# A hybrid decoder layer on one core: the last tile's RWKV tail factored ahead of its norm, four of its output weights in another ring, and the query's token rows on ScalarE's queue

## The chip, the core and the metric

The kernel runs on one core of one Trainium2 chip. A core has five engines with an instruction queue each: TensorE (PE in the profile; its weight loads are PEld), VectorE (DVE), ScalarE (ACT), GpSimd (POOL) and SyncE (SP). Each works through its own queue in order and waits on semaphores. SP, ACT and POOL also issue the DMA transfers. The metric is the device time of one execution in microseconds (us). Before the change it is 3875.11 us, the median of three runs (3873.53, 3875.11 and 3887.86).

## What is computed

One layer of a hybrid decoder, for 1024 prompt tokens and 64 sample tokens (8 sequences of 8), model width 1024. Cut to what matters here:

```python
xn = rmsnorm(h, norm_mix)
proj = xn @ w_in                                # retention columns | RWKV-7 columns
o_ret = head_norm(o_ret, GN_EPS) * silu(g_ret)  # retention, chunks of 128 tokens
gate = sigmoid(fg) @ rw_g2
o_rw = head_norm(o_rw, RWKV_LN_EPS) * rw_ln_g + rw_ln_b
o_rw = o_rw + jnp.sum(r4 * k4 * rw_rk, axis=-1, keepdims=True) * v4
o_rw = o_rw * gate
h = h + jnp.concatenate([o_ret, o_rw], axis=-1) @ w_out
# peer: 8 heads, 2 x 128 keys, the best 16 of each, 16 experts of 16384 per token and head
q = (rmsnorm(h, norm_ffn) @ wq)                 # query, scores against keys, top 16
h = h + sum over experts of gelu(xn . u[e]) * softmax(score) * v[e]
h = h + sigmoid(rmsnorm(h, ple_norm) @ ple_gate) * (p_l @ ple_proj)
y = rmsnorm(h, norm_final)
```

The three lines of `o_rw` that follow the head norm are the ones that the change factors in another way.

## The kernel before, in words

The tokens are cut into nine tiles: 0 to 7 of 128 prompt tokens, and 8 with the 64 sample tokens. The program's author writes generators (a `yield` ends each piece), and a scheduler puts the pieces of all of them into one fixed order for each engine. So the order is not written out by hand: a change of a ring, of a buffer's size or of an engine can move work that has nothing to do with it, also far from the place. All on-chip tiles come from rings: a tag with `bufs` slots. A new tile waits until the reader of the slot's last owner is done; a pool that is laid over the memory of a closed pool waits for its readers in the same way.

The stages, in the order of the program:

- **Projections** (`group_a`) and **mixers** (`ret_mix`, `rw_mix`), tile by tile in the order 0, then 1, 8, 2, 3, 4, 5, 6, 7 (`BORDER`, in `group_b`). The RWKV chain carries a state from tile to tile, so tile 7 ends it. `rw_mix` ends with `py` (the outputs of the 8 heads, in PSUM), the head norm (`head_norm`, L403 to L420), and L970 to L984: times `lng` (L972), plus `lnb` (L973), plus the bonus term `bv` (L975, L976), times the gate `p` (L978 is the matmul, tile `pgt`). For tile 7 the result stays on the chip as `self.tail` (L980, L981), in the ring `Wq`; all of it is VectorE's.
- **Output rows** (`c_rows`, L572 to L631): the rows of `od` are loaded (`cot`), transposed (`etr`, `coT`), multiplied with `w_out` (tiles `cw`, matmuls `ewo`), added to `x` (`ch`), normed with `norm_ffn` (`cgr` holds its row), and written to `xd` in DRAM. For the last tile (`da` is given) all eight `cw` of 128x1024 are loaded into slots of the rings `uh` and `ul` (L581), `ch` into a slot of `uraw`, and the normed rows are split and transposed straight into the query's operand.
- **Early experts** (`early`, `gather`): for tiles 0, 1 and 8 the expert rows are gathered row by row by an indirect DMA that POOL issues (`grow`, L1130), 512 KB a step, and VectorE multiplies them: first with the token (L1144), then into the sum (L1158, tile `gacc`). These steps run all through the mixers and the query, one tile after another. They are put into the order as filler between other work. The early query of a tile uses the ring `Wq` (four slots of 128x1024) for its weights.
- **Query** (`c_query`) for tiles 2 and 3 (operand `x1`) and 4 to 7 (`x`): `rows_in` loads the token rows from `xd` (`cxn`, L1002, a ring of two), transposes them (`ntr`, L321) and splits them into two fp32r parts (`cx`: ScalarE L298, VectorE L300). Then for 16 blocks: weights `wqr` are loaded by SP into `uraw`, split into `wqh` and `wql` (ScalarE, POOL), multiplied (`pq`), scored (`psc`), and the best 16 are picked by VectorE (L1035 to L1039).
- **Gates and hidden units** of tiles 4 to 7 (dense), gathers for tiles 2 and 3, then the dense second half (`py`, L1303), and the last stage (`ple`) with the final norm.

The place of the change is the seam between mixers and query. SP's queue holds there, one behind the other: the token rows `cxn`, the eight `cw`, `ch`, `wqr` and `cgr`. The pool `da` with `uh`, `ul` and `uraw`, and the pool `cn` with `cxn`, are laid over memory that the mixers used.

Of the kernel before, what the change touches and what calls it, by code (L numbers as in the profile page):

```python
# [8 lines left out]
F32 = mybir.dt.float32  # L9
# [5 lines left out]
OP = mybir.AluOpType  # L15
AX = mybir.AxisListType

D = 1024
# [145 lines left out]
UB = 2  # L164
# [15 lines left out]
DW = 4  # L180
# [6 lines left out]
PGT = "a"  # L187
# [7 lines left out]
QB = 4  # L195
# [5 lines left out]
def spans(tiles):  # L201

    e = [sum(SIZE[t] for t in tiles[:i]) for i in range(len(tiles) + 1)]
    return dict(zip(tiles, e)), e[-1]
# [8 lines left out]
class K:  # L213
# [357 lines left out]
    def c_rows(self, wp, t, ring=4, da=None, x=None):  # L571

        nc, I = self.nc, self.I
        n = SIZE[t]
        half = lambda name: wp.tile([128, 512], F32, name=name, tag="x2k", bufs=ring)
        cs = [slice(0, 512), slice(512, 1024)]
        if da is not None:
            ws = []
            for k in range(8):
                ws.append(da.tile([128, D], F32, name="cw", tag=("uh", "ul")[k % 2], bufs=DW))  # L580
                nc.sync.dma_start(ws[k], I['w_out'][k])  # L581
        if da is not None:
            h = da.tile([128, D], F32, name="ch", tag="uraw", bufs=UB)
        else:
            h = wp.tile([128, D], F32, name="ch", tag="sr", bufs=1)
        nc.sync.dma_start(h[:n], I['x'][t * 128:t * 128 + n])
        yield
        ot = [half("cot"), self.tail if t == 7 else half("cot")]
        oT = [wp.tile([128, 4, 128], F32, name="coT", tag="qm", bufs=2) for _ in range(2)]
        for k in range(1 if t == 7 else 2):  # L590
            nc.sync.dma_start(ot[k][:n], self.od[t][:n, cs[k]])
        yield
        for k in range(2):
            p = self.ps("etr", "a").rearrange("p (a b) -> p a b", a=4)
            for j in range(4):
                nc.tensor.transpose(p[:, j, :n], ot[k][:n, j * 128:j * 128 + 128], self.c("ident")[:n, :n])
            nc.scalar.activation(oT[k][:, :, :n], p[:, :, :n], AF.Copy)
            yield
        if da is not None:
            p = [self.ps("ewo", "b") for _ in range(2)]  # L600
            for k in range(8):
                for c in range(2):
                    nc.tensor.matmul(p[c][:n], oT[k // 4][:, k % 4, :n], ws[k][:, cs[c]], start=k == 0, stop=k == 7)
            for c in range(2):
                nc.vector.tensor_tensor(h[:n, cs[c]], p[c][:n], h[:n, cs[c]], op=OP.add)
        else:
            for c in range(2):
                p = self.ps("ewo", "a")
                for k in range(8):
                    w = half("cw")  # L610
                    nc.sync.dma_start(w, I['w_out'][k, :, cs[c]])
                    nc.tensor.matmul(p[:n], oT[k // 4][:, k % 4, :n], w, start=k == 0, stop=k == 7)  # L612
                    if k % 4 == 3:
                        yield
                nc.vector.tensor_tensor(h[:n, cs[c]], p[:n], h[:n, cs[c]], op=OP.add)
        nc.scalar.dma_start(self.hd[t][:n], h[:n])
        junk = wp.tile([128, D], BF, name="csq", tag="x2k", bufs=ring)
        ssq = wp.tile([128, 1], F32, name="cssq")
        nc.scalar.activation(junk[:n], h[:n], AF.Square, accum_out=ssq[:n])
        r = self.rsq(wp, ssq, n, 1.0 / D, 1e-6, 1, "crs")  # L620
        gr = [half("cgr") for _ in range(2)]
        o = ROWS['norm_ffn'][0]
        for c in range(2):
            nc.sync.dma_start(gr[c], I['rows'][o + 512 * c:o + 512 * c + 512].partition_broadcast(128))
            nc.vector.scalar_tensor_tensor(h[:n, cs[c]], h[:n, cs[c]], r[:n], gr[c][:n], op0=OP.mult, op1=OP.mult)
        if x is not None:
            self.split_T(h, n, x[0], x[1], 0)
        else:
            nc.scalar.dma_start(self.xd[t][:n], h[:n])
        self.rowed.add(t)  # L630
        yield  # L631
# [64 lines left out]
    def rw_mix(self, t):  # L696
        nc, I, O, wp = self.nc, self.I, self.O, self.cw
        smp = t == 8
        n, o = SIZE[t], t * 128
# [3 lines left out]
        hb = "bd" if smp or first else "bb"  # L703
        T2 = lambda name: wp.tile([128, 4 * n], F32, name=name, tag="t2", bufs=6)
        T3 = lambda name: wp.tile([128, 512], F32, name=name, tag="t3", bufs=4)
# [7 lines left out]
        p = self.ps("pz")  # L713
# [8 lines left out]
        sf13 = wp.tile([128, 128], F32, name="sf13", bufs=b2)  # L722
# [3 lines left out]
        for k in range(2):  # L726
            p = self.ps("pcs")[:, :258].rearrange("p (a b) -> p a b", a=2)
# [10 lines left out]
        p = self.ps("pa").rearrange("p (a b) -> p a b", a=4)  # L738
# [21 lines left out]
        p = self.ps("pbon")  # L760
# [3 lines left out]
        bon = wp.tile([128, 16], F32, name="bon", bufs=b2)  # L764
# [24 lines left out]
        for src, dst in ((nbt, Q), (kt, Kq)):  # L789
            for k in range(2):  # L790
# [6 lines left out]
                for s in range(2):  # L797
# [4 lines left out]
                    else:  # L802
                        for j in range(2):
                            h = 2 * (2 * k + j) + s
# [3 lines left out]
        for nm, src in (("vtk", vT), ("nbk", nbt), ("ktk", kt)):  # L808
            d = wp.tile([128, 512], F32, name=nm, bufs=b2)
# [21 lines left out]
        for li, m in enumerate(LEVELS):  # L831
# [4 lines left out]
            for s in range(2):  # L836
                p = self.ps("trz", hb[s]).rearrange("p (a b) -> p a b", a=4)
# [4 lines left out]
                p = self.ps("pG", hb[s])[:, :256].rearrange("p (h q) -> p h q", h=4)  # L842
# [5 lines left out]
            for s in range(2):  # L848
                p = self.ps("pZG", hb[s])[:, :256].rearrange("p (h q) -> p h q", h=4)
# [11 lines left out]
        def state_mm(p, hp, j):  # L861
            pr = p[:n, hp * 128:hp * 128 + 128]
            if smp:
                return self.seq_state(self.co, art[:, hp, j, :64], I['s_wkvT'], hp)
            elif not first:
                nc.tensor.matmul(pr, art[:, hp, j, :n], S0[:, hp, :], start=True, stop=False)

        V = toks["vtk"]
        hq = lambda h: (h % 2) * 4 + h // 2
        p = self.ps("pX", "d")  # L870
        for hp in range(4):
            sq = state_mm(p, hp, 0)
            for s in range(2):
                h = 2 * hp + s
# [8 lines left out]
        if smp:  # L883
            p = self.ps("pU", "d")
# [5 lines left out]
        else:  # L890
            lo, up = slice(0, 64), slice(64, 128)
            for half in (lo, up):
                if half is up:
                    p = self.ps("pL", "d")
# [5 lines left out]
                p = self.ps("pU", "d")  # L900
# [5 lines left out]
        if not smp:  # L906
            p = self.ps("pS", "d").rearrange("p (a b) -> p a b", a=4)
# [15 lines left out]
            if t == 7:  # L923
                p = self.ps("pso", "d").rearrange("p (a b) -> p a b", a=4)
# [7 lines left out]
        else:  # L932
# [6 lines left out]
            for h in range(8):  # L939
                hs = slice(h * 64, h * 64 + 64)  # L940
                p = self.ps("pss", "b")
# [16 lines left out]
        for hp in range(4):  # L958
            sq = state_mm(py, hp, 1)
            for s in range(2):  # L960
                h = 2 * hp + s
                hs = slice(h * 64, h * 64 + 64)
                if smp:
                    self.seq_mm(py[:n, hs], *sq, s)
                nc.tensor.matmul(py[:n, hs], Kq[:n, hq(h), 1, :n], V[:n, hs], start=first, stop=False)
                nc.tensor.matmul(py[:n, hs], Q[:n, hq(h), 1, :n], U[:n, hs], start=False, stop=first or smp or s == 1)
            if hp % 2:
                yield
        xc = self.head_norm(wp, py, n, 64e-5, T3)
        xf = xc.rearrange("p h d -> p (h d)")  # L970
        eng = nc.vector if t == 7 else nc.gpsimd
        eng.tensor_tensor(xf[:n], xf[:n], self.lng[:n], op=OP.mult)  # L972
        eng.tensor_tensor(xf[:n], xf[:n], self.lnb[:n], op=OP.add)  # L973
        bv = T3("bv").rearrange("p (h d) -> p h d", h=8)
        nc.vector.tensor_tensor(bv[:n], V[:n].rearrange("p (h d) -> p h d", h=8), bon[:n, 8:16, None].to_broadcast([n, 8, 64]), op=OP.mult)  # L975
        eng.tensor_tensor(xc[:n], xc[:n], bv[:n], op=OP.add)  # L976
        p = self.ps("pgt", PGT or hb[0])
        nc.tensor.matmul(p[:n], sf13[:, :n], self.g2, start=True, stop=True)  # L978
        if t == 7:
            self.tail = self.ep0.tile([128, 512], F32, name="tail", tag="Wq", bufs=QB)  # L980
            nc.vector.tensor_tensor(self.tail, xf, p, op=OP.mult)  # L981
        else:
            nc.vector.tensor_tensor(xf[:n], xf[:n], p[:n], op=OP.mult)
            nc.scalar.dma_start(self.od[t][:n, 512:], xf[:n])  # L984

# [10 lines left out]
    def rows_in(self, wp, tiles, x):  # L996

        off, _ = spans(tiles)
        for t in tiles:
            n = SIZE[t]  # L1000
            xn = wp.tile([128, D], F32, name="cxn", bufs=CN)
            self.nc.sync.dma_start(xn[:n], self.xd[t][:n])  # L1002
            self.split_T(xn, n, x[0], x[1], off[t])
            yield

# [552 lines left out]
```

## Time and profile before

| | |
|---|---|
| median of three runs | 3875.11 us |
| the profiled execution's own time | 3881.51 us |
| its span (first to last instruction) | 3879.7 us |
| busy in the span: PE, PEld, DVE, ACT, POOL | 86%, 71%, 77%, 31%, 61% |
| mean granted TensorE clock | 0.883 of full speed |
| read and written in HBM | 986.68 MB, 95.94 MB |
| gather steps of 512 KB (L1130) | 1152 |
| tail of tile 7 ready (L981 ends) | 1767.8 us |
| first query matmul of tiles 4 to 7 | 1840.6 us |

How to read the rows below. A row of the chain gives the start in us from the span's start, the length, and what ran; the chain is followed back from the last instruction, each step to what released it. A row of the timeline gives start, length, engine, line, operation and shape, and in brackets the idle time before it. A row of the waits gives who waited for whom: us in total, times, the longest. A row of the DMA issues gives the queue, the count, the size of one, and the median us from issue to landing. The table by stretches gives busy us of each engine, the granted clock, the DMA engines' share and what they moved. The lines that carry the prediction are shown in it.

### The profile page before, as it was taken

The numbers are of one execution on the slowest core, as the hardware profiler recorded it, in microseconds if no ns is written. First come the engines' busy times: TensorE is split into PE (matmuls) and PEld (weight loads), VectorE is DVE, ScalarE is ACT, GpSimd is POOL, SyncE is SP. The second block draws the span as 40 slices with busy tenths as digits, with TensorE's granted clock in tenths as the row PEclk, the third lists the DMA queues.
The fourth block names the chain that finished last, engine by engine and source line by source line (L and its number), as shares of the span: only waits on it lengthen the run. The fifth ranks groups of instructions, "written<-read, shape, count | busy, mean of one in ns | idle before, by whom it ended". The sixth has DMA issues, their size and how long they took to land.

```text
span 3879.7 us, 52665 instructions
## 1 busy us (share of the span) xinstructions
PE 3346.4 (86%) x17749; PEld 2748.3 (71%) x17749; DVE 2984.9 (77%) x5884; ACT 1220.5 (31%) x2247; POOL 2361.5 (61%) x2059
## 2 busy tenths in 40 slices
PE   7789995868779878883999989999899989899979
PEld 7688894645747757662887767887688766677757
DVE  4454388877787697876998999977777777788875
ACT  4232220111111111211232626777533333333322
POOL 5363176454365365554569888875688787777740
PEclk9799995667868567876999999999899999999989
DMA  7266558899778878889779888998999999999962
GB/s 249 74 218 208 172 179 285 279 300 296 231 243 285 294 264 272 290 288 327 223 261 309 298 289 316 315 349 320 346 339 339 336 361 359 358 352 345 334 223 72
DMA packets 457320, 1086.23 MB, mean 280 GB/s; under 512 B 73627, under 2 KB 176281, under 8 KB 452378
## 3 DMA queue, kind: packets, MB, share of 16 engines
q0 software_dynamic: 165888, 604.05, 44.4%
q1 hardware_dynamic: 236638, 382.77, 31.0%
q10 hardware_dynamic: 54524, 96.03, 6.6%
q8 instruction: 141, 2.31, 0.2%
q14 instruction: 129, 1.06, 0.1%
HBM read 986.68 MB, written 95.94 MB: 279 GB/s over the span
## 4 chain that ended last, share of the span: by engine, by line
PE 37%; DVE 24%; DMA 12%; POOL 8%; issue 8%; ACT 3%; ACTq 0%; SPq 0%; POOLq 0%; DVEq 0%
PE py L1303 13%; DVE grow L1144 6%; POOL grow L1130 4%; DMA grow<-in_pu,eid 4%; DVE gacc L1158 3%; DMA grow<-in_pv,eid 3%; PE ph L327 2%; PE ph L329 2%; PE ph L328 2%; POOL vl L302 2%; PE epq L1198 2%; DMA ft<-fd 2%; DVE eq L1085 2%; PE ewo L612 2%; DVE oh L1245 1%
## 5 line engine op out<-in xcount | busy, mean ns | idle before, releaser
L1130 POOL DMA_INDIRECT grow<-in_pv,eid x576 | 572.0, 993 | 497.4 <-DVE gacc L1158 310.2
L1130 POOL DMA_INDIRECT grow<-in_pu,eid x576 | 573.3, 995 | 432.5 <-DVE grow L1144 257.9
L1158 DVE SCALAR_TENSOR_TENSOR gacc<-grow,ac,gacc 128x1024 f32<-128x1024 f32 x571 | 732.2, 1282 | 51.1 <-DMA grow<-in_pv,eid 46.3
L1144 DVE SCALAR_TENSOR_TENSOR grow<-grow,gacc 128x1024 f32<-128x1024 f32 x576 | 690.3, 1213 | 87.8 <-DMA grow<-in_pu,eid 77.2
L1303 PE MATMUL py<-ah,vl 128*128 128x512 f32 x1024 | 410.0, 403 | 40.6 <-POOL vl L302 40.0
L1303 PE MATMUL py<-ah,vh 128*128 128x512 f32 x1024 | 406.9, 398 | 16.1 <-ACT vh L298 9.5
L329 PE MATMUL ph<-cx,ul 128*128 128x512 f32 x1024 | 406.5, 398 | 14.4 <-POOL ul L302 14.3
L327 PE MATMUL ph<-cx,uh 128*128 128x512 f32 x1024 | 408.6, 399 | 5.4 <-ACT uh L298 3.6
L328 PE MATMUL ph<-cx,uh 128*128 128x512 f32 x1024 | 406.2, 397 | 0.0
L1303 PE MATMUL py<-al,vh 128*128 128x512 f32 x1024 | 405.0, 396 | 0.0
L302 POOL TENSOR_TENSOR vl<-vraw,vh 128x640 fp32r<-128x640 f32 (+2 forms) x224 | 325.5, 1457 | 33.3 <-ACT vh L298 29.6
L302 POOL TENSOR_TENSOR ul<-uraw,uh 128x1024 fp32r<-128x1024 f32 x128 | 308.0, 2406 | 53.5 <-ACT uh L298 50.9
L1303 PEld LDWEIGHTS py<-ah,vl 128*128 128x128 f32 x1024 | 193.4, 189 | 108.0 <-POOL vl L302 67.0
L298 ACT ACTIVATE vh<-vraw 128x640 fp32r<-128x640 f32 (+2 forms) x224 | 154.5, 692 | 356.4 <-PE py L1303 173.8
L1307 DVE TENSOR_TENSOR yT<-yT,py 128x512 f32<-128x512 f32 x216 | 147.7, 685 | 127.7 <-PE py L1303 126.9
L1303 PEld LDWEIGHTS py<-ah,vh 128*128 128x128 f32 x1024 | 194.5, 190 | 69.2 <-ACT vh L298 21.9
L329 PEld LDWEIGHTS ph<-cx,ul 128*128 128x128 f32 x1024 | 194.7, 190 | 60.6 <-POOL ul L302 20.9
L327 PEld LDWEIGHTS ph<-cx,uh 128*128 128x128 f32 x1024 | 194.9, 190 | 46.7 <-ACT uh L298 5.3
L298 ACT ACTIVATE uh<-uraw 128x1024 fp32r<-128x1024 f32 x128 | 135.2, 1057 | 286.9 <-DMA uraw<-in_puT 144.3
L1303 PEld LDWEIGHTS py<-al,vh 128*128 128x128 f32 x1024 | 193.8, 189 | 44.2
L328 PEld LDWEIGHTS ph<-cx,uh 128*128 128x128 f32 x1024 | 195.3, 191 | 39.3
L1245 DVE TENSOR_TENSOR oh<-csta,pit 128x512 f32<-128x512 f32 x256 | 162.3, 679 | 43.1 <-PE pwt L1250 42.9
(400 smaller groups left out, 7806.7 us busy)
## 6 DMA issues: line engine op xcount, KB each, us to landing
uraw<-in_puT SPq DMA_DIRECT2D x128, 512.0 KB, 4.7
vraw<-in_pvd SPq DMA_DIRECT2D x152, 320.0 KB, 5.9
cw<-in_w_out SPq DMA_DIRECT2D x128, 256.0 KB, 5.2
wd<-wst ACTq DMA_DIRECT2D x28, 1024.0 KB, 15.2
wt<-wd SPq DMA_DIRECT2D x64, 448.0 KB, 7.6
wraw<-in_w_ret SPq DMA_DIRECT2D x48, 512.0 KB, 4.9
ewq<-in_wq SPq DMA_DIRECT2D x48, 512.0 KB, 5.1
gd<-geh ACTq DMA_DIRECT2D x96, 256.0 KB, 5.2
```

The lines of the kernel that those rows point to most:

```text
L298: nc.scalar.activation(hi, src, AF.Copy)
L302: nc.gpsimd.tensor_tensor(lo, src, hi.bitcast(F32), op=OP.subtract)
L327: mm(out, lh(k), rh(k), start=first and k == 0, stop=False)
L328: mm(out, lh(k), rl(k), start=False, stop=False)
L329: mm(out, ll(k), rh(k), start=False, stop=last and k == nk - 1)
L612: nc.tensor.matmul(p[:n], oT[k // 4][:, k % 4, :n], w, start=k == 0, stop=k == 7)
L1130: nc.gpsimd.indirect_dma_start(out=g, out_offset=None, in_=src, in_offset=bass.IndirectOffsetOnAxis(ap=self.eid[t][:, j:j + 1], axis=0))
L1144: nc.vector.scalar_tensor_tensor(g[:, c], g[:, c], 1.0, x[:, c], op0=OP.mult, op1=OP.mult, accum_out=hv[:, i, j:j + 1])
L1158: nc.vector.scalar_tensor_tensor(y[:, c], g[:, c], ac[:, j:j + 1], y[:, c], op0=OP.mult, op1=OP.add)
L1245: nc.vector.tensor_tensor(oh[j], io, p[:, j, s + b:s + b + 4, None].to_broadcast([128, 4, 128]), op=OP.is_equal)
L1303: nc.tensor.matmul(p, lh[:, b, :], rh, start=b == 0 and j == 0, stop=b == nb - 1 and j == 2)
L1307: nc.vector.tensor_tensor(yT[:, d, :], yT[:, d, :], p, op=OP.add)
```

## The change

Three edits.

1. In `rw_mix`, for tile 7 alone, the gate's matmul is issued before the head norm, and two tiles are worked out ahead: `gg = lng * p` and `bg = (V * bon + lnb) * p`. After the norm two steps are left, `xf * gg` and `+ bg`. `gg` and `bg` take slots of the ring `t2`. The tail's tile moves from the ring `Wq` to the slot `xT`. For the other tiles nothing changes but the line numbers.
2. In `c_rows`, for the last tile, the first four `cw` take the four slots of the ring `Wq`, and the other four go on taking two slots each of `uh` and `ul`. `ch` moves from `uraw` to the slot `sr`, as for the other tiles.
3. In `rows_in`, the loads of `cxn` are issued by ScalarE's queue in place of SP's.

```diff
@@ c_rows
             for k in range(8):
-                ws.append(da.tile([128, D], F32, name="cw", tag=("uh", "ul")[k % 2], bufs=DW))
+                if k < QB:
+                    ws.append(self.ep0.tile([128, D], F32, name="cw", tag="Wq", bufs=QB))
+                else:
+                    ws.append(da.tile([128, D], F32, name="cw", tag=("uh", "ul")[k % 2], bufs=DW))
                 nc.sync.dma_start(ws[k], I['w_out'][k])
-        if da is not None:
-            h = da.tile([128, D], F32, name="ch", tag="uraw", bufs=UB)
-        else:
-            h = wp.tile([128, D], F32, name="ch", tag="sr", bufs=1)
+        h = wp.tile([128, D], F32, name="ch", tag="sr", bufs=1)
@@ rw_mix
+        gate = lambda: nc.tensor.matmul(p[:n], sf13[:, :n], self.g2, start=True, stop=True)
+        if t == 7:
+            p = self.ps("pgt", PGT or hb[0])
+            gate()
+            gg = T2("gg")
+            bv = T2("bg")
+            nc.vector.tensor_tensor(gg, self.lng, p, op=OP.mult)
+            b3 = bv.rearrange("p (h d) -> p h d", h=8)
+            nc.vector.tensor_tensor(b3, V.rearrange("p (h d) -> p h d", h=8), bon[:, 8:16, None].to_broadcast([n, 8, 64]), op=OP.mult)
+            nc.vector.tensor_tensor(bv, bv, self.lnb, op=OP.add)
+            nc.vector.tensor_tensor(bv, bv, p, op=OP.mult)
         xc = self.head_norm(wp, py, n, 64e-5, T3)
         xf = xc.rearrange("p h d -> p (h d)")
...
         if t == 7:
-            self.tail = self.ep0.tile([128, 512], F32, name="tail", tag="Wq", bufs=QB)
-            nc.vector.tensor_tensor(self.tail, xf, p, op=OP.mult)
+            nc.vector.tensor_tensor(xf, xf, gg, op=OP.mult)
+            self.tail = self.ep0.tile([128, 512], F32, name="tail", tag="xT")
+            nc.vector.tensor_tensor(self.tail, xf, bv, op=OP.add)
@@ rows_in
-            self.nc.sync.dma_start(xn[:n], self.xd[t][:n])
+            self.nc.scalar.dma_start(xn[:n], self.xd[t][:n])
```

What this does to the order of the engines, at the places of which the prediction speaks. First VectorE, behind the subtraction of the mean (`hnx<-pY,hns`) up to tile 7's tail; `gacc` are gather steps of tile 1. Before:

```order
L975 TENSOR_TENSOR bv<-vtk,bon 128x512
L417 TENSOR_REDUCE hnss<-hnq 128x8
L1158 SCALAR_TENSOR_TENSOR gacc<-grow,ac,gacc 128x1024 x2
L419 TENSOR_TENSOR hnx<-hnx,hnr 128x512
L1158 SCALAR_TENSOR_TENSOR gacc<-grow,ac,gacc 128x1024
L972 TENSOR_TENSOR hnx<-hnx,row_ln_g 128x512
L1158 SCALAR_TENSOR_TENSOR gacc<-grow,ac,gacc 128x1024
L973 TENSOR_TENSOR hnx<-hnx,row_ln_b 128x512
L1158 SCALAR_TENSOR_TENSOR gacc<-grow,ac,gacc 128x1024
L976 TENSOR_TENSOR hnx<-hnx,bv 128x512
L1158 SCALAR_TENSOR_TENSOR gacc<-grow,ac,gacc 128x1024
L981 TENSOR_TENSOR tail<-hnx,pgt 128x512
```

The same place now (the gather steps are L1169 in the changed file):

```order
L413 TENSOR_TENSOR hnx<-pY,hns 128x512
L417 TENSOR_REDUCE hnss<-hnq 128x8
L1169 SCALAR_TENSOR_TENSOR gacc<-grow,ac,gacc 128x1024 x2
L419 TENSOR_TENSOR hnx<-hnx,hnr 128x512
L1169 SCALAR_TENSOR_TENSOR gacc<-grow,ac,gacc 128x1024
L983 TENSOR_TENSOR hnx<-hnx,gg 128x512
L985 TENSOR_TENSOR tail<-hnx,bg 128x512
```

From the last norm row of tile 6 (`ch<-ch,crs,cgr`, a little further up) to the tail there stood nine gather steps and, behind `hnx<-pY,hns`, seven others; now there are seven gather steps and four others. The four steps that make `gg` and `bg` stand further up, between the last updates of `Z` and the chain's `X`. Counted from the program's start, 450 gather steps stand ahead of the tail before and 443 now; ahead of the query's first pick (L1035) it is 479 and 471, ahead of its last pick 527 and 519, and ahead of the first sum of the dense half (`yT`) 775 and 776.

Second SP's queue at the seam. Before:

```order
L591 DMA cot<-od_99 128x512
L1002 DMA cxn<-xd_85 128x1024
L1002 DMA cxn<-xd_86 128x1024
L581 DMA cw<-in_w_out 128x1024 x8
L586 DMA ch<-in_x 128x1024
L1002 DMA cxn<-xd_87 128x1024
L1013 DMA wqr<-in_wq 128x1024
L1002 DMA cxn<-xd_88 128x1024
L1002 DMA cxn<-xd_89 128x1024
L1013 DMA wqr<-in_wq 128x1024 x3
L624 DMA cgr<-in_rows 128x512 x2
```

Now:

```order
L591 DMA cot<-od_99 128x512
L586 DMA ch<-in_x 128x1024
L584 DMA cw<-in_w_out 128x1024 x4
L1024 DMA wqr<-in_wq 128x1024 x4
L1147 DMA gx<-xd_91 64x1024 x2
L1024 DMA wqr<-in_wq 128x1024
L624 DMA cgr<-in_rows 128x512 x2
```

The five `cxn` are gone from it, four of the eight `cw` too, and the token rows of tile 8's gather (`gx`) have come in, which stood far ahead before. The other four `cw` now stand inside the output rows of tiles 3 and 4, where SP loads the halves of `w_out` for those:

```order
L591 DMA cot<-od_95 128x512
L611 DMA cw<-in_w_out 128x512 x12
L584 DMA cw<-in_w_out 128x1024 x3
L611 DMA cw<-in_w_out 128x512 x4
L445 DMA qv<-rd_126 128x2048
```

Before, the sixteen L611 of tile 3 stood there in one piece. Third ScalarE, from tile 6's last row to the tail's transposed copy (`coT`). Before:

```order
L629 DMA xd_89<-ch 128x1024
L415 ACTIVATE hnq<-hnx 128x512
L298 ACTIVATE cx_13020<-ntr 128x4x128 x4
L298 ACTIVATE cx_13025<-ntr 128x4x128 x4
L597 ACTIVATE coT<-etr 128x512
L298 ACTIVATE wqh<-wqr 128x1024
```

Now:

```order
L415 ACTIVATE hnq<-hnx 128x512
L1013 DMA cxn<-xd_85 128x1024
L1013 DMA cxn<-xd_86 128x1024
L298 ACTIVATE cx_13022<-ntr 128x4x128 x2
L1013 DMA cxn<-xd_87 128x1024
L298 ACTIVATE cx_13022<-ntr 128x4x128 x2
L1013 DMA cxn<-xd_88 128x1024
L298 ACTIVATE wqh<-wqr 128x1024 x2
L298 ACTIVATE cx_13027<-ntr 128x4x128 x2
L1013 DMA cxn<-xd_89 128x1024
L298 ACTIVATE cx_13027<-ntr 128x4x128 x2
L597 ACTIVATE coT<-etr 128x512
```

The loads of the token rows now stand between the copies that empty the transposes, each behind those whose slot it takes, and two splits of query weights (`wqh`) stand ahead of tile 4's copies. The first of these loads has a new wait: the memory of `cxn` lies over the ring `t2`, in which `gg` and `bg` now live until the tail's last step, so it waits for that step. Before, the last owners of that memory were steps far ahead of it.

More of the change, by code (lines that the diff above doesn't have):

```diff
@@ L968, in rw_mix @@
                 yield
+        gate = lambda: nc.tensor.matmul(p[:n], sf13[:, :n], self.g2, start=True, stop=True)
[9 more added lines that the diff above has]
+            nc.vector.tensor_tensor(bv, bv, p, op=OP.mult)
         xc = self.head_norm(wp, py, n, 64e-5, T3)
         xf = xc.rearrange("p h d -> p (h d)")
[L971 to L978, printed above, removed]
         if t == 7:
-            self.tail = self.ep0.tile([128, 512], F32, name="tail", tag="Wq", bufs=QB)
-            nc.vector.tensor_tensor(self.tail, xf, p, op=OP.mult)
-        else:
+            nc.vector.tensor_tensor(xf, xf, gg, op=OP.mult)
+            self.tail = self.ep0.tile([128, 512], F32, name="tail", tag="xT")
+            nc.vector.tensor_tensor(self.tail, xf, bv, op=OP.add)
+        else:
+            nc.gpsimd.tensor_tensor(xf[:n], xf[:n], self.lng[:n], op=OP.mult)
+            nc.gpsimd.tensor_tensor(xf[:n], xf[:n], self.lnb[:n], op=OP.add)
+            bv = T3("bv").rearrange("p (h d) -> p h d", h=8)
+            nc.vector.tensor_tensor(bv[:n], V[:n].rearrange("p (h d) -> p h d", h=8), bon[:n, 8:16, None].to_broadcast([n, 8, 64]), op=OP.mult)
+            nc.gpsimd.tensor_tensor(xc[:n], xc[:n], bv[:n], op=OP.add)
+            p = self.ps("pgt", PGT or hb[0])
+            gate()
             nc.vector.tensor_tensor(xf[:n], xf[:n], p[:n], op=OP.mult)
```

## The prediction

> **What bounds the kernel now.** I read the table by stretches first, to see which engine sets the pace on both sides of the change. Columns: the stretch, its length, busy us (and count) of PE, PEld, DVE, ACT and POOL, then granted clock, DMA share and GB/s.
>
> ```profile
> core 0: us, PE busy (x) PEld busy (x) DVE busy (x) ACT busy (x) POOL busy (x), PEclk, DMA share, GB/s
> 1640.00:1747.00 107.00, 90.22 (x486) 69.92 (x484) 85.91 (x106) 14.05 (x24) 55.79 (x56) 0.79 0.85 287
> 1747.00:1768.00 21.00, 1.63 (x8) 1.23 (x8) 18.70 (x23) 1.23 (x2) 11.97 (x12) 0.50 0.94 333
> 1768.00:1842.00 74.00, 32.43 (x113) 20.00 (x114) 43.98 (x43) 13.19 (x20) 36.31 (x34) 0.64 0.90 325
> 1842.00:1960.00 118.00, 118.00 (x727) 105.57 (x727) 115.47 (x529) 36.02 (x62) 60.55 (x48) 1.00 0.70 221
> 1960.00:2160.00 200.00, 187.35 (x878) 154.78 (x877) 183.27 (x676) 65.79 (x97) 161.81 (x122) 0.98 0.87 292
> 2160.00:2400.00 240.00, 217.06 (x1019) 175.58 (x1018) 223.61 (x366) 121.05 (x215) 202.80 (x146) 0.99 0.87 296
> 2400.00:2560.00 160.00, 154.45 (x802) 128.92 (x801) 152.27 (x285) 114.81 (x231) 129.47 (x98) 1.00 0.93 335
> 2560.00:2760.00 200.00, 176.46 (x937) 151.10 (x936) 154.34 (x258) 157.23 (x344) 117.80 (x91) 0.92 0.93 334
> ```
>
> From 1842 to 1960, in the query, PE is busy for all 118.00 us: whatever brings the query's start forward is kept in full there. From 1747 to 1842, the seam, PE works 34 of 95 us. So the change is aimed at a hole of about 61 us of PE. Next I followed the chain that ended last through the hole.
>
> ```profile
> 1767.20 0.60 DVE tail L981
> 1767.93 7.02 DMA cw<-in_w_out
> 1775.02 18.75 DMA cxn<-xd
> 1793.90 1.95 PE ntr L321 x8
> ...
> 1802.17 6.22 PE ewo L603 x8
> ...
> 1819.18 5.54 DMA wqr<-in_wq
> ...
> 1829.50 9.41 DMA cgr<-in_rows
> ...
> 1839.84 1.09 PE ntr L321 x4
> ```
>
> The tail ends at 1767.8. Only then do seven of the eight `cw` leave, the token rows of tile 4 stand behind them in SP's queue and land 26 us after the tail, and with them come the transposes and the two halves of `ewo`. The waits in this stretch say the same:
>
> ```profile
> SPq L581 <- DVE tail L981: 19.0, 1, 19.0
> PE ntr L321 <- DVE tail L981: 19.4, 1, 19.4
> PE ntr L321 <- DMA cxn<-xd: 15.6, 2, 14.8
> DVE gacc L1158 <- DMA grow<-in_pv,eid: 20.4, 15, 4.6
> ```
>
> SP held its queue 19.0 us for the tail, and PE lost 19.4 us to the tail (the gate `pgt` and the transposes share a ring in PSUM) and 14.8 to the late rows. VectorE for its part waited 20.4 us for gathered rows: at 0.90 to 0.94 DMA share the seam is also short of transfer.
>
> **The change part by part.** All terms are against the profiled execution (3881.5 us). T is the end of the tail.
>
> *A, the way to T.* The steps at the tail, with the gather steps between them:
>
> ```profile
> 1726.04 0.42 DVE L853 TENSOR_TENSOR Z<-Z,pZG 128x256 f32<-128x256 f32 x1 [0.99 <-PE pZG L851]
> 1730.22 0.69 DVE L899 TENSOR_TENSOR X<-X,pL 64x512 f32<-64x512 f32 x1 [1.24 <-PE pL L897]
> 1760.18 1.28 DVE L1158 SCALAR_TENSOR_TENSOR gacc<-grow,ac,gacc 128x1024 f32<-128x1024 f32 x1
> 1761.38 0.69 DVE L972 TENSOR_TENSOR hnx<-hnx,row_ln_g 128x512 f32<-128x512 f32 x1
> 1767.10 0.68 DVE L981 TENSOR_TENSOR tail<-hnx,pgt 128x512 f32<-128x512 f32 x1
> ```
>
> A gather step takes 1.20 us from its start to the next (1760.18 to 1761.38), an elementwise step 0.6. By the new order two gather steps and three others less stand between the norm row and T: 2 x 1.20 + 3 x 0.60 = 4.2 us. The four new steps (4 x 0.68 = 2.7 us) stand where VectorE waits for PE (0.99 and 1.24 in the rows above), which hides most of them; without that cover they cost 2.7. Four gather steps less stand ahead of tile 7 already, worth up to 4.8 us if VectorE set the pace; it is busy 86 of 107 us from 1640, so I take 2. A is **-6**, between -9 and -3.
>
> *B, from T to the query.* The prices:
>
> ```profile
> cw<-in_w_out SPq DMA_DIRECT2D x8, 512.0 KB, 11.7
> cxn<-xd SPq DMA_DIRECT2D x5, 512.0 KB, 11.7
> hd<-ch ACTq DMA_DIRECT2D x1, 512.0 KB, 9.0
> xd<-ch ACTq DMA_DIRECT2D x1, 512.0 KB, 7.8
> hd<-ch ACTq DMA_DIRECT2D x1, 512.0 KB, 3.5
> DMA packets 1322, 4.79 MB, mean 399 GB/s; under 512 B 152, under 2 KB 152, under 8 KB 1322
> 1840.58 0.99 PE L327 MATMUL pq<-cx,wqh 128*128 128x512 f32 x2
> ```
>
> Now, at T, SP sends three `cw` and two `wqr`, ScalarE the rows of tiles 2 and 3; the first of these has to wait for T too, since `gg` and `bg` hold the memory that it lands in. A load on ScalarE's queue beside a busy SP took 3.5, 7.8 and 9.0 us; I take 9. Transposes and copies of two tiles end near T+12, about as before, and the next loads leave between T+8 and T+12. But ScalarE has two `wqh` ahead of tile 4's copies, and they wait for `wqr`. Nine transfers of 0.524 MB on SP's queue (seven `cw`, `ch`, `cxn`) took from 1767.9 to 1793.8, that is 183 GB/s; three `cw` and two `wqr` are 2.62 MB, 14 us alone, 20 with ScalarE's 1.05 MB in between. I take 18, add two splits and the copies, and have tile 4's operand at T+21 in place of 1796.5, T+28.7. That is 8 us. Behind it the two `ewo` stand as before. `cgr` leaves earlier, since both slots of `uraw` now serve `wqr`; but VectorE's row step was held until 1837.4 by a gathered row anyway, and until 1838.9 by `cgr`, so 1 us. B is **-9**.
>
> Bytes bound it: 74 us at 325 GB/s are 24.0 MB. Four `cw` less, two `cxn` more, `gx` in and `ch` out leave 23.0 MB: 71 us at 325, 58 at 399, the highest rate shown. So B lies between -3 and -16.
>
> *Waits that are added.* Behind the first `cxn` on ScalarE's queue stand the copies of the transposes that need it; PE needs those, and nothing else is late for it. Behind `gx` on SP, which waits for the tail's transposes (slot `xT`), stand one `wqr` and `cgr`; the transposes come ahead of `ewo`, and `cgr` is needed after it: nothing.
>
> *C, the query.* Same work, PE full: 0.
>
> *D, gather steps put off.* Eight steps less are done by the first pick, and nine more stand between the last pick and the dense half. The price of one in the seam:
>
> ```profile
> L1158 DVE SCALAR_TENSOR_TENSOR gacc<-grow,ac,gacc 128x1024 f32<-128x1024 f32 x27 | 34.8, 1287 | 16.5 <-DMA grow<-in_pv,eid 15.9 <-DVE gacc L1158 0.3
> ```
>
> Nine at 1.29 us are 11.6 us of VectorE. From 1960 to 2760 it is idle for 86 of 800 us and PE for 65, so neither has much room, nor is one alone the bound. Bounds: 0 if the steps fill idle time, 25 at the distance that they keep in the seam (74 / 27 = 2.74 us). I take **+5**, under half of the busy price, because both engines have holes there.
>
> *E, four `cw` ahead.* 2.1 MB, 5.3 us at 399 GB/s, in the output rows of tiles 3 and 4. There SP's loads run behind PE anyway:
>
> ```profile
> 1343.37 38.23 SPq L611 DMA_DIRECT2D cw<-in_w_out  x16
> ```
>
> Sixteen half loads are spread over 38 us, paced by the ring. The third of the new ones also waits for the last picks of tile 8's early query, with four half loads behind it. Between 0 and 5; I take **+1**, since there is slack in the ring's pace.
>
> The sum is -6 - 9 + 0 + 5 + 1 = -9: 3872.5 for the profiled execution. The median of the runs shown lies 6.4 us below that execution (3875.1 against 3881.5), so I predict **3866**.
>
> **The rivals.**
>
> *1, more than that.* The put-off gather steps fill idle time (2560 to 2760 has 46 us of it on VectorE) and the seam runs at the highest rate shown: -7 - 16 + 0 + 1 = -22, 3853. For it: the longest gap of PE is a queue's order, not a rate. Against: 0.90 DMA share.
>
> *2, the queue gains nothing.* The token rows leave earlier but the same bytes pass the same engines, so the seam ends when they have passed: B is -3, the sum -6 - 3 + 5 + 1 = -3, 3872. For it: the shares of 0.94 and 0.90. Against: 325 GB/s there beside 399 in its best part. The Trainium skill states this rule ("DMA: Bandwidth & Descriptors", section "Issuing engines are not separate DMA queues"): transfers started by different engines run on the same 16 DMA engines, and several issuers save only issue time. By it alone B would be its lower end. The same page, in "Queues, rings and completion order", has the engines take turns between queues packet by packet, which would let a row on ScalarE's queue pass SP's weights. The trace agrees with the second in that `xd` landed in 7.8 us on ScalarE's queue beside loads on SP's, where a row behind the weights took 18.75; that the total does not rise no run here shows yet.
>
> *3, slower.* The put-off gather steps come back at the full distance of 2.74 us each, between 1960 and 2760, where they stand in VectorE's order ahead of steps on which PE waits: +25. With A and B at their lower ends and E at 3 it is -3 - 3 + 25 + 3 = +22, 3897. It decides as soon as a step put off costs more than what A and B save, 15 us by my terms, that is 1.7 us a step. For it: VectorE at 93% and PE at 95% from 1960 to 2560. Against: the holes after 2560.
>
> **How the numbers follow.** The forecast has 0.36, rival 1 0.30, rival 2 0.21, rival 3 0.13. About 0.5% (19 us) is what a measurement of this kernel can tell from no change: below 3855.7 is faster, which only rival 1 reaches, 0.30; above 3894.5 is slower, rival 3, 0.13; the forecast and rival 2 lie between, 0.57. The range is 3846 to 3890: it takes in the forecast and rivals 1 and 2 with their bounds (the terms' best ends give -9 - 16 = -25, 3850) and leaves out most of rival 3.
>
> **What would show it.** A: the tail ends about 6 us earlier, with `hnx<-hnx,gg` right ahead of it. B: no `cxn` lands later than some 10 us after its issue, PE's wait for it shrinks from 15.6 us, and the first `pq` of tiles 4 to 7 comes near 1826 instead of 1840.6; if ScalarE's copies of tile 4 wait for `wqh`, the weights are the new bound there. D: the first gate step (`oh`) or the first sum into `yT` gains less than the query's start did; rival 1 has it gain as much, rival 3 has it come later than before. E: tile 3's and 4's `ewo` wait longer for `cw`. The prediction is wrong at its root if the tail comes later than 1767.8, or if the order's changes outside of the seam, which begin near 1270 us, move the time by more than these terms.

## The result, and the profile after

The change makes the kernel a little slower. Its median is 3896.48 us (six runs, 3883.47 to 3904.4) against 3873.2 us before (six runs, 3868.01 to 3887.86): ratio 1.0051, 95% interval 1.0032 to 1.007. Measured a second time it gave 1.0025 (1.0007 to 1.0043). The forecast was 3866 and the range ended at 3890. The profiled execution took 3895.1 us (span 3893.3), 13.6 more than that of before.

The table by stretches of the changed kernel, with the columns and edges of the one before:

```profile
1747.00:1768.00 21.00, 3.91 (x16) 3.13 (x16) 13.38 (x15) 2.39 (x4) 8.02 (x8) 0.50 0.97 371
1768.00:1842.00 74.00, 53.06 (x243) 39.04 (x244) 54.11 (x94) 17.28 (x28) 44.83 (x39) 0.82 0.88 308
1842.00:1960.00 118.00, 118.00 (x733) 105.76 (x732) 118.00 (x596) 37.90 (x64) 58.25 (x43) 1.00 0.65 203
2160.00:2400.00 240.00, 215.97 (x986) 174.80 (x987) 208.96 (x376) 110.49 (x188) 205.46 (x153) 0.98 0.87 295
2400.00:2560.00 160.00, 152.96 (x794) 128.74 (x793) 142.52 (x248) 110.91 (x224) 131.49 (x92) 0.98 0.91 327
2560.00:2760.00 200.00, 161.85 (x859) 140.14 (x857) 153.81 (x257) 153.36 (x343) 102.37 (x83) 0.89 0.89 325
```

Read the second row first. Between 1768 and 1842 PE now works 53.06 us in place of 32.43: the query has moved into the hole, as it should. Then read the rows from 2160 on. PE works less in each of them than before (215.97 against 217.06, 152.96 against 154.45, 161.85 against 176.46), and VectorE too. So the gain is made in the seam and lost in the gates stage, where PE and VectorE have more idle time than before.

The edits did what they say. The timeline of the changed kernel has the tail with `gg` and `bg` behind one gather step:

```profile
1747.69 1.28 DVE L1169 SCALAR_TENSOR_TENSOR gacc<-grow,ac,gacc 128x1024 f32<-128x1024 f32 x1
1748.88 0.69 DVE L983 TENSOR_TENSOR hnx<-hnx,gg 128x512 f32<-128x512 f32 x1
1749.60 0.69 DVE L985 TENSOR_TENSOR tail<-hnx,bg 128x512 f32<-128x512 f32 x1
```

Its waits and DMA issues have the token rows on ScalarE's queue:

```profile
PE ntr L321 <- DMA cxn<-xd: 27.9, 3, 21.0
```

```profile
cxn<-xd ACTq DMA_DIRECT2D x5, 512.0 KB, 7.8
```

A row of tokens now lands 7.8 us after its issue in place of 11.7, and PE no longer waits for the tail itself (19.4 us before). But PE's wait for the rows grew from 15.6 to 27.9 us: the first load has to wait for the tail.

For the rest one table of milestones does more than a chain. Each number is the start of a row of VectorE's timeline (tail and last sum: its end): the tail, the first pick of tiles 2 to 7 (L1035), the first gate step `oh` (L1245), the first and the last sum into `yT` (L1305, L1307). "Steps" are the gather steps between `oh` and the first sum. Counted by these rows, 452 steps start ahead of the tail before and 445 in the change, 481 and 473 ahead of the first pick, 537 and 529 ahead of the last pick, 779 and 780 ahead of the first sum; the first part of this document has each of these 2 to 10 lower, with the same differences, and the argument rests on the differences. The runs below the line are the experiments of the next section.

| kernel | tail | to pick | to `oh` | to first sum (steps) | to last sum | to the end |
|---|---|---|---|---|---|---|
| before | 1767.8 | 77.5 | 297.5 | 630.6 (201) | 934.0 | 172.3 |
| before, again | 1761.2 | 79.8 | 297.6 | 632.1 (201) | 932.2 | 170.6 |
| the change | 1750.3 | 71.5 | 299.4 | 658.8 (209) | 943.4 | 169.9 |
| the change, again | 1767.7 | 70.6 | 299.8 | 655.8 (209) | 936.4 | 169.7 |
| --- | | | | | | |
| edit 1 alone | 1749.7 | 81.9 | 301.6 | 638.8 (203) | 934.1 | 171.2 |
| edit 2 alone | 1761.4 | 73.4 | 305.7 | 632.4 (203) | 939.0 | 171.0 |
| edit 3 alone | 1757.0 | 77.8 | 302.0 | 632.4 (198) | 930.7 | 174.2 |
| edits 1 and 2 | 1741.5 | 71.9 | 299.9 | 657.3 (209) | 933.6 | 171.6 |
| 8 steps left out | 1761.2 | 69.5 | 299.0 | 635.2 (201) | 924.7 | 171.3 |
| 24 late steps left out | 1737.9 | 70.7 | 299.9 | 659.6 (209) | 930.9 | 160.4 |
| half of VectorE's part | 1752.2 | 73.1 | 274.2 | 641.5 (205) | 934.8 | 175.1 |
| half of the bytes too | 1738.1 | 69.6 | 302.7 | 615.3 (239) | 926.2 | 163.7 |
| 33 steps moved late | 1744.5 | 72.6 | 300.6 | 654.9 (209) | 929.8 | 175.3 |
| edit 3, 33 moved late | 1755.2 | 77.7 | 301.7 | 629.4 (198) | 918.7 | 171.5 |

The fourth column is the result. The stage takes 655 to 660 us in all five profiles with 209 steps, and 629 to 639 in all seven with 198 to 203. It is the only column in which the change is later than before by far more than the profiles of one kernel differ; in the column from tail to pick it is as clearly earlier, 71.5 and 70.6 against 77.5 and 79.8.

What passes in that stage is shown by the DMA answer for it. q0 is the queue of the gathers. Before, from 2142.8 to 2773.4:

```profile
DMA packets 59783, 200.09 MB, mean 317 GB/s; under 512 B 6296, under 2 KB 9880, under 8 KB 56152
...
q0 software_dynamic: 28728, 104.61, 46.1%
```

The change, from 2121.2 to 2780.0:

```profile
DMA packets 61525, 206.17 MB, mean 313 GB/s; under 512 B 6489, under 2 KB 10073, under 8 KB 57894
...
q0 software_dynamic: 30178, 109.89, 46.9%
```

The rate is nearly the same, and 6.1 MB more pass, 5.3 of them on the gathers' queue. At 315 GB/s 6.1 MB are 19 of the 28 us, an estimate from these rows; what the other 9 are is not shown. The stretch as a whole, before:

```profile
2142.80:2773.40 630.60, 578.57 (x2903) 481.35 (x2902) 556.75 (x960) 408.68 (x819) 473.23 (x349) 0.97 0.90 317
```

The change:

```profile
2121.20:2780.00 658.80, 587.08 (x2904) 490.08 (x2903) 559.60 (x988) 409.26 (x820) 487.93 (x359) 0.95 0.89 313
```

In 28.2 us more, VectorE is busy 2.9 us longer and PE 8.5. VectorE's idle time in the stage grows from 73.9 to 99.2 us and PE's from 52.0 to 71.7. The lower granted clock, 0.95 in place of 0.97, does not explain it: the kernel with eight steps left out, further down, has 0.95 too and takes 635.2 us. Nor did VectorE's part of the gather steps grow by as much. Its groups in that stage, before:

```profile
L1144 DVE SCALAR_TENSOR_TENSOR grow<-grow,gacc 128x1024 f32<-128x1024 f32 x128 | 152.2, 1213 | 10.0 <-DMA grow<-in_pu,eid 9.9
L1158 DVE SCALAR_TENSOR_TENSOR gacc<-grow,ac,gacc 128x1024 f32<-128x1024 f32 x72 | 92.1, 1279 | 3.6 <-DMA grow<-in_pv,eid 3.1
```

The change:

```profile
L1155 DVE SCALAR_TENSOR_TENSOR grow<-grow,gacc 128x1024 f32<-128x1024 f32 x133 | 158.8, 1213 | 11.6 <-DMA grow<-in_pu,eid 11.6
L1169 DVE SCALAR_TENSOR_TENSOR gacc<-grow,ac,gacc 128x1024 f32<-128x1024 f32 x74 | 94.8, 1281 | 15.3 <-DMA grow<-in_pv,eid 14.7
```

Busy time rises by 9.3 us (253.6 against 244.3), and VectorE's idle time in front of gathered rows by 13.3 (26.9 against 13.6). The largest single part of VectorE's idle time in the stage is put down to PE, before and in the change:

```profile
DVE oh L1245 <- PE pwt L1250: 42.9, 28, 4.5
```

```profile
DVE oh L1256 <- PE pwt L1261: 45.8, 34, 3.9
```

PE's longest wait there is in turn for ScalarE's copy of `oh`, 30.8 us before and 40.7 in the change. So several engines wait for one another in this stage, and the gathered rows are one part of it.

### The profile page after: what moved, and what is told of

The parts are those of the page before. It is cut to its first block, busy times and chain, and to the rows that moved or that the text cites. A ratio compares the mean times of both kernels' runs of the same rounds, so it can differ in the third digit from the quotient of the medians.

```text
span 3893.3 us, 52668 instructions
## 1 busy us (share of the span) xinstructions
PE 3352.3 (86%) x17749; PEld 2760.4 (71%) x17749; DVE 2984.2 (77%) x5885; ACT 1222.1 (31%) x2247; POOL 2364.9 (61%) x2059
## 5 line engine op out<-in xcount | busy, mean ns | idle before, releaser
L1169 DVE SCALAR_TENSOR_TENSOR gacc<-grow,ac,gacc 128x1024 f32<-128x1024 f32 x571 | 732.5, 1283 | 72.2 <-DMA grow<-in_pv,eid 67.5
L1256 DVE TENSOR_TENSOR oh<-csta,pit 128x512 f32<-128x512 f32 x256 | 162.2, 680 | 45.9 <-PE pwt L1261 45.8
```

What stands on the lines that cost most here:

```text
L1169: nc.vector.scalar_tensor_tensor(y[:, c], g[:, c], ac[:, j:j + 1], y[:, c], op0=OP.mult, op1=OP.add)
L1256: nc.vector.tensor_tensor(oh[j], io, p[:, j, s + b:s + b + 4, None].to_broadcast([128, 4, 128]), op=OP.is_equal)
```

## The experiments

Theory P: the steps that the new order puts off pass through the gates stage at the distance that the steps keep there, so the stage is longer by that distance for each. Rivals: V, a put-off step costs VectorE's busy time alone; S, the seam's gain is kept and something else loses; O, it is the re-made order of the stage and not the number of steps; G, the dense half too goes at the steps' distance, so that the time follows the number of steps ahead of the last sum.

**Each edit by itself.** Each of the first three kernels takes one hunk group of the diff above; the fourth takes edits 1 and 2, so that against the full change it differs only in

```diff
-            self.nc.scalar.dma_start(xn[:n], self.xd[t][:n])
+            self.nc.sync.dma_start(xn[:n], self.xd[t][:n])
```

> Edit 1 alone (gate, gg and bg ahead; tail in slot xT). In its order 4 gather steps fewer than before stand ahead of the query's last pick (533 against 537 of 1152) and 2 more ahead of the last sum into yT (1135 against 1133). Theory G, the gather steps run at their own pace and the time follows how many stand ahead of the last sum into yT, 2.8 us each as in the dense half of the profile before: +6 us, ratio 1.0015, and the first query pick earlier than 1845 without a gain at the end. Rival S, the seam's gain is kept and only the other edits lose: -6 us or better, ratio 0.9985. Rival V, a step put off costs VectorE's busy 1.29 us: -6 + 5 = -1, ratio 1.000.

> Edit 2 alone (four cw in the ring Wq, ch in slot sr). No gather step is put off (537 ahead of the last pick as before, 1136 against 1133 ahead of the last sum into yT). G: 3 steps at 2.8 us, +8 us, ratio 1.002. S and V: it gains what the four earlier cw save behind the tail, 3 to 9 us, ratio 0.998 to 0.999. If the four cw in the query ring cost the output rows something (term E), the stretch from 1240 to 1640 is longer by 1 to 5 us.

> Edit 3 alone (token rows on ScalarE's queue). Two gather steps more than before stand ahead of the last pick, three fewer ahead of the last sum into yT (1130 against 1133). G: -8 us, ratio 0.998. S: the rows pass the weights, first query matmul of tiles 4 to 7 about 5 to 8 us earlier than 1840.6 and all of it kept, ratio 0.998. The two differ in the seam: under G the end moves by 8 whether or not the query starts earlier. If bytes alone decide (the same page of bytes on the same engines), the query starts when it did.

> Edits 1 and 2 without 3. VectorE's order is that of the full change, instruction for instruction (529 gather steps ahead of the last pick, 1137 ahead of the last sum into yT); only SP's and ScalarE's queues differ. G: the same time as the full change whatever the seam does, ratio 1.004 to 1.006. S: without edit 3 the query starts later than in the full change (1821.8 at the first pick) by the wait for the rows, 5 to 15 us, and the end is later by as much: ratio 1.007 to 1.009.

Measured: edit 1 1.0029 (1.001 to 1.0047), edit 2 1.0014 (0.9997 to 1.003), edit 3 0.997 (0.9951 to 0.9989), edits 1 and 2 1.0038 (1.0021 to 1.0056). S falls for edits 1 and 2: neither is faster. G has the sign of all four and nearly the sizes, so I took it further. But in the table the stage from the first gate step to the first sum is what differs, 657.3 us where 209 steps stand in it and 632 to 639 where 198 to 203 do; G's own stretch, the dense half, lies between 930.7 and 939.0 in no order of the steps. Only edits 1 and 2 together put eight steps off (edit 1 alone four of them), and they together have the longer stage.

Two things in these four runs P does not explain. Edit 1 alone is slower by 11 us with only two steps more in the stage: behind the tail its profile is 15 us longer than before, 7 of them in this stage, 4 between pick and `oh` and 3 between tail and pick. And among the kernels with 198 to 203 steps the length does not follow the number: 198 steps took 632.4 us, 201 took 630.6, 632.1 and, further down, 635.2, 203 took 638.8 and 632.4. So a price of one step is at most an average over the eight.

Edit 3 brings the query no nearer: 77.8 us from tail to pick alone, where before has 77.5 and 79.8; and 71.5 and 70.6 with it against 71.9 without it beside the other edits. The DMA answer for that stretch, edits 1 and 2 (1741.5 to 1813.4):

```profile
DMA packets 6710, 23.84 MB, mean 332 GB/s; under 512 B 767, under 2 KB 767, under 8 KB 6707
```

The full change (1750.3 to 1821.8):

```profile
DMA packets 6591, 23.42 MB, mean 327 GB/s; under 512 B 752, under 2 KB 752, under 8 KB 6588
```

Before (1767.8 to 1845.3):

```profile
DMA packets 7050, 25.18 MB, mean 325 GB/s; under 512 B 780, under 2 KB 780, under 8 KB 7047
```

Two queues move no more than one: 327 GB/s against 332. This is the rule of the Trainium skill that rival 2 set beside its own rows ("DMA: Bandwidth & Descriptors", section "Issuing engines are not separate DMA queues": starting transfers from several engines saves no more than issue time), and these rows agree with it. With the full change 1.8 MB less pass in the seam, which at 325 GB/s is 5.4 of the 6.0 us; 1.0 of it is missing on the queues of the loads and stores and 0.7 on the gathers'. Which edit does it is shown by the table: edit 2 alone, with four `cw` less behind the tail, has 73.4 us from tail to pick, and edit 1 alone has 81.9. Why edit 3 alone is faster stays open: its tail stands at 1757.0 and 1755.2, 4 to 13 us ahead of before's, which is less than one order's own scatter (last section).

**Steps and their price.** Four kernels, all on the full change. The first two leave steps out, tile 1's last 8 and tile 3's last 24:

```diff
-        for j in range(n):
+        for j in range(n - (8 if t == 1 else 0)):
```

The next two leave out half of the columns in the steps of tiles 8 and 2, on VectorE first and then also in the loads:

```diff
+        if t in (8, 2):
+            cs = [slice(0, D // 2)]
...
-            nc.gpsimd.indirect_dma_start(out=g, out_offset=None, in_=src,
+            nc.gpsimd.indirect_dma_start(out=g[:, :W], out_offset=None, in_=src.rearrange('e (a b) -> (e a) b', b=W) if W < D else src,
```

> The full change, with the last 8 steps of tile 1's second pass (rows of v) left out, 1144 gather steps in all. Its order is that of the change up to the first gate step (571 steps ahead), then 201 gather steps stand between the first gate step and the first sum into yT, as in before, in place of 209. Theory P, the gates stage passes at the gather steps' distance (659 us for 209 steps in the change, 631 for 201 before, 3.15 each): the stage takes 633 us, the end comes 25 us earlier than in the full change, ratio to before 0.998 to 0.999. Theory V, a step costs VectorE's 1.29: 10 us earlier, ratio 1.002. Theory O, the re-made order of the stage costs the time, not the steps: ratio 1.004 to 1.005 as the full change.

> The full change, with the last 24 steps of tile 3's second pass left out, 1128 in all. The order up to the first sum into yT is that of the change; ahead of the last sum into yT stand 1128 steps in place of 1137. Theory G, the dense half passes at the gather steps' distance (2.8 each): 25 us earlier, ratio 0.998. Theory P, only the gates stage goes by the steps, and the dense half is PE's: 0 to 5 us earlier, ratio 1.003 to 1.005.

> The full change, with the gather steps of tiles 8 and 2 multiplying only the first 512 of 1024 columns (0.68 in place of 1.29 us of VectorE each); the loads stay whole. 205 steps stand between the first gate step and the first sum into yT in place of 209. If VectorE sets the distance of the steps there: 205 x 0.6 = 120 us of room, the stage falls from 659 us to 560 or less. If the loads set it: 205 x 3.15 = 646 us, as long as it was step for step.

> As the run before, and the loads of these steps fetch 256 KB in place of 512 KB too. 239 steps stand between the first gate step and the first sum into yT. If the moved bytes set the distance: below 2.8 us a step, the stage near or below 620 us though 30 steps more are in it. If the issue on GpSimd or the step's place in VectorE's order sets it: 3.1 us a step, 740 us.

Measured, in this order: 0.9943 (0.9922 to 0.9964), 0.9982 (0.9962 to 1.0002), 0.993 (0.9904 to 0.9955), 0.9898 (0.9865 to 0.993).

With 8 steps left out the stage takes 635.2 us, where P said 633 and V and O 649 and 659. The order of the rest is the change's, so O falls. Its DMA answer (2129.7 to 2764.9) is back at before's:

```profile
DMA packets 59878, 200.42 MB, mean 316 GB/s; under 512 B 6311, under 2 KB 9895, under 8 KB 56247
...
q0 software_dynamic: 28796, 104.86, 46.5%
```

The whole run gained more than P's 25 us, 32 to 42 by the ratios; 13 of it stand in the dense half (924.7 against 937.8, the mean of the change's two profiles and of edits 1 and 2), for which the runs have no explanation. Six steps fewer start there (352 in place of 358), but edit 3 alone has 352 as well and takes 930.7.

With VectorE's part of the steps halved the stage takes 641.5 us for 205 steps, 3.13 a step, where the change has 3.15. (The work beside the steps is not quite the same: 3004 matmul records stand in it in place of 2904.) Its groups and its stretch (2099.5 to 2741.0):

```profile
L1158 DVE SCALAR_TENSOR_TENSOR grow<-grow,gacc 128x512 f32<-128x512 f32 x137 | 90.8, 678 | 24.6 <-DMA grow<-in_pu,eid 24.4
L1172 DVE SCALAR_TENSOR_TENSOR gacc<-grow,ac,gacc 128x512 f32<-128x512 f32 x66 | 49.4, 748 | 28.9 <-DMA grow<-in_pv,eid 28.4
```

```profile
2099.50:2741.00 641.50, 593.17 (x3004) 497.94 (x3003) 465.34 (x1003) 415.03 (x830) 496.54 (x363) 0.97 0.90 323
```

```profile
DVE oh L1259 <- PE pwt L1264: 81.6, 42, 4.6
```

VectorE is busy 465.34 us in place of 559.60, and most of what it saved turned into waiting: 52.8 us for gathered rows in place of 26.9, and 81.6 for PE in place of 45.8, as the last row shows. The stage is far from the 560 us or less that would have shown VectorE to set the distance, and leaving out eight steps gave 22 us in this stage and not 10. So V falls: in this stage VectorE's time is not what a step costs. The bytes pass here at 323 GB/s, so the 313 to 317 of the other kernels shown are no ceiling. VectorE's time does count elsewhere: between pick and `oh`, where VectorE is full with picks, this kernel is 26 us faster (274.2). With the bytes halved as well the stage takes 615.3 us with 34 steps more in it, 2.57 a step:

```profile
2110.40:2725.70 615.30, 572.68 (x2915) 482.95 (x2915) 470.05 (x1001) 412.43 (x820) 513.59 (x388) 0.97 0.76 258
```

What the edit changes between these two kernels is the size of the loads (and with it the order), so the loads have a part in the price, and GpSimd's issue of them does not set it, for which 740 us were expected. The rate of the DMA engines alone is not it either: they are down to 0.76 busy, and still VectorE waits longer for gathered rows than before, 100.6 us against 52.8:

```profile
DVE grow L1159 <- DMA grow<-in_pu,eid: 54.3, 50, 5.0
DVE gacc L1173 <- DMA grow<-in_pv,eid: 46.3, 31, 3.2
```

Nor is 2.57 us the price of a step: it is the stage's length over its steps, and PE is busy 572.68 of the 615.3 us. How much of a step's 3.1 us is its bytes, how much the time from issue to landing and how much the waits of the engines for one another, these runs do not separate.

Leaving out tile 3's last steps fitted G (0.998) and not P, but the table says why that decides nothing: the dense half is 7 us shorter and the last stage 10, since the gathers that ran beside it until 3765.5 now end at 3687.

**G against P, without leaving anything out.** The last 33 steps of tile 3 are bound to memory of the last stage:

```diff
+            g = self.lp.tile([128, D], F32, name="lrow", bufs=4) if self.lp else slot("grow", rows[j % len(rows)])
...
+                            g = self.behind(self.gather(gp, t, acc=acc), PG)
+                            if t == G1[-1]:
+                                for _ in range(255 - LATE):
+                                    next(g)
...
+                self.lp = sb("plt", e, bufs=2, side="right")
+                run(g)
+                self.ple(dl, self.lp, yT)
```

> The full change, with the last 33 of tile 3's gather steps bound to memory that is free only after the dense half, so that they run beside the last stage, where the DMA engines are 0.3 busy. Nothing is left out. 1119 steps stand ahead of the last sum into yT in place of 1137; up to the first sum into yT the order is that of the change. Theory G (the dense half too passes at the steps' distance): 18 x 2.8 = 50 us earlier than the full change, ratio 0.992. Theory P (only the gates stage goes by the steps; the dense half is PE's): ratio 1.004 to 1.005, as the full change. If the late steps hold up the last stage, which ends 168 us after the last sum into yT, that stretch is longer than 168.

> Edit 3 alone with the same 33 steps late. 581 gather steps ahead of the first gate step, 198 from there to the first sum into yT, 1119 ahead of the last in place of 1130. G: 11 x 2.8 = 31 us earlier than edit 3 alone (0.997), ratio 0.989. P: 0.997.

> The full change once more, as the base of the others: ratio 1.003 to 1.007. Its second profile shows how far the tail's end moves from run to run with one and the same order; theory P has 655 to 662 us for the 209 steps of the gates stage again, whatever the tail does.

> The kernel before once more, for a second profile: ratio 1. Theory P has 628 to 635 us for its 201 steps between the first gate step and the first sum into yT, and the tail's end tells how much of the 17.5 us by which it came earlier in the change's profile is the change's.

Measured: 1.0027 (1.0007 to 1.0048) on the full change, which in the same series has 1.0025 (1.0007 to 1.0043); 0.9968 (0.9948 to 0.9989) on edit 3, which alone had 0.997. G falls: 18 steps fewer ahead of the last sum change nothing. The dense half is 8 us shorter (929.8 against 937.8), and the last stage 5 longer (175.3 against 169.9 and 169.7). On edit 3 the profile has the dense half 12 us shorter (918.7 against 930.7), where G had 31, and the ratio does not show it. The second profiles repeat the stage: 655.8 us for 209 steps, 632.1 for 201. Edit 3, with or without the late steps, is the only version here that leaves nothing out and is shown to be faster than before, by 0.3%.

## Why the prediction failed, step by step

- **A, the way to the tail (-6): not resolved.** The tail ended at 1767.8 and 1761.2 before; in eight profiles with the change's order on VectorE up to the tail it ended between 1737.9 and 1767.7, on average 1749.2. That is 15 us earlier than 1764.5, more than forecast, with a spread of 30 for one order. It goes with the granted clock in the mixers: from 1240 to 1500 that was 0.61 in both profiles of before, 0.67 or 0.68 in the six of the eight whose tail ended by 1752.2, and 0.63 and 0.59 in the two at 1761.2 and 1767.7. So how much of the 15 us is the change's stays open.
- **B, from the tail to the query (-9): right in size by luck, wrong in the reason.** 71.2 us on average in those eight profiles against 78.65, so -7.5. I had it from the queue of the token rows. Without edit 3 the stretch is as short (71.9 us), and edit 2 alone has 73.4, so it is edit 2, with four `cw` less behind the tail. Rival 2 had the mechanism of edit 3 right, nothing, but its B of -3 was too small: it had 1.0 MB less, and 1.8 MB less passed. The three rows that gave 9 us for a load on ScalarE's queue are stores (`hd<-ch`, `xd<-ch`); the loads then took 7.8 us.
- **C, the query (0): nearly right.** 299.7 us from pick to `oh` in the change, the mean of its two profiles and of edits 1 and 2, against 297.6: +2.
- **D, the steps put off (+5): the step that failed.** The five profiles with 209 steps average 657.3 us, the two of before 631.4: +26 us, 3.2 for each of the eight; with eight left out it is 635.2, 2.8 each. The prediction took less than VectorE's busy price of 1.29 "because both engines have holes there". The holes did not take the steps in: with the steps VectorE's idle time in the stage grew from 73.9 to 99.2 us and PE's from 52.0 to 71.7. VectorE's busy time was not the price, since with half of it the stage took 641.5 us; smaller loads made the stage shorter with more steps in it, so the loads have a part in it, and the rows of that stage had their DMA share of 0.87 to 0.93 beside the holes. What else makes up the price is open.
- **E, four `cw` ahead (+1):** no sign of a cost. With edit 2 alone the tail ends at 1761.4, not later than before's.
- **Rival 3** had the price (25 for nine) and the place, and it came about; its deciding point, 1.7 us a step, was passed. That its total of 3897 lies next to the first median, 3896.48, is in part luck: its A and B were smaller than what was measured, and it had nothing for the dense half. Its reason, that the steps stand in VectorE's order ahead of steps on which PE waits, no run here tests by itself. It gives PE 95% from 1960 to 2560; by its own rows that is 93% (558.9 of 600 us).

With the averages the sum is -15 - 7.5 + 2 + 26, then +5 in the dense half (937.8 against 933.1) and -1 behind it: +9 us. The two measurements say +10 (1.0025) and +20 (1.0051). The sum reaches the first, and the scatter of the tail alone covers the second; what the rest consists of, if it is there at all, is open. So is the loss with edit 1 alone, which has only two steps more in the gates stage.

So the seam did become shorter, and the gates stage gave back more than that. The order of the steps is fixed when the program is built: eight fewer stand ahead of the first pick, none of them comes back in the query (56 steps start from the first pick to the last before, and 56 in the change), and eight more stand between `oh` and the first sum. Why the scheduler puts them there no run here asks.

## What to carry to other kernels

Where a long stream of transfers runs beside all stages, an edit that shortens one stage can move a part of the stream into another. Count the steps at each milestone before and after, and look at those that move in the stage in which they arrive: its bytes and its waits, and not only the busy time or the holes of the engine that uses the data. Idle time of an engine is no cover as long as it is not known what the engine waits for: here the idle time grew with the steps. The price is best measured by leaving the moved steps out.

## What the runs showed that was not expected

The same order of instructions on VectorE up to the tail gave tails 30 us apart. In one pair it can be followed to the mixers. The stretch from 1240 to 1500, the change:

```profile
1240.00:1500.00 260.00, 216.40 (x1049) 177.62 (x1048) 213.02 (x529) 37.32 (x85) 141.84 (x137) 0.67 0.83 282
```

The change again:

```profile
1240.00:1500.00 260.00, 218.35 (x964) 179.86 (x963) 199.44 (x502) 35.34 (x82) 131.90 (x129) 0.59 0.78 266
```

At a clock of 0.59 in place of 0.67 PE is as busy and gets 964 matmul records done in place of 1049; the tail of the second came 17.4 us later. In a single pair of profiles such a shift reads like a gain in the seam: of the 17.5 us by which the change's tail came earlier, this pair alone could not have told how much is the change's. The lengths between two milestones behind it repeat within 5 us up to the first sum, for one order with whole steps, and they are what the reading here rests on.
